# Refining the keys' norms once per head and token, and spreading them to channels by TensorE

## The chip, the cores and the metric

One core of a Trainium2 chip runs the whole program. The metric is device microseconds from start to end of one execution, as the median of several runs; lower is better. TensorE (PE in the rows) multiplies matrices from SBUF into PSUM, VectorE (DVE) and ScalarE (ACT) work on both memories, GpSimd (POOL) on SBUF, and SyncE (SP) issues most of the transfers.

## What is computed

The kernel runs two layers of a backbone over 1024 latent and 256 context tokens. The part that matters here is in the second layer, ahead of a recurrence (RWKV-7): each head's keys, 64 channels wide, are scaled by `k_k` and divided by their norm over those 64 channels.

```python
k = token_shift_mix(k, mu[1])
kk = heads(k * k_k).astype(jnp.float32)
kk = kk / jnp.maximum(jnp.sqrt(jnp.sum(kk * kk, axis=-1, keepdims=True)), 1e-12)
...
    s_fin, o = wkv_scan(r_h, heads(decay), k_d, v_h, -kk, kk * a_h, init, reverse=(d == 1))
```

There are 8 heads, so one norm per head and token: 8 x 1280 numbers.

## The kernel before, in words

Channels lie on partitions and tokens along the row, so a tile of 128 partitions holds a pair of heads (64 channels each) and 1280 columns: 1024 latent tokens, then 256 of the context. The stage `odd_in` goes over four such pairs, j = 0 to 3. For each pair, `dense` projects keys, values and receptances (i = 0, 1, 2). A dense block is 24 matmuls, eight triples of a split-precision product (`hi`/`lo` weights and inputs, one `wl` and two `wh` rows in the trace); blocks are 512, 512 and, for keys and values, 256 columns wide. After the four pairs come four more projections of 1024 columns (`ex` in the rows), each ended by `gates`: load a gate from memory, multiply (L1037), store (`ZCD`).

For each projected tile `shift` mixes neighbouring tokens: GpSimd adds the two neighbours into a buffer `both` (L1061), VectorE scales and adds (L1063, L1066). Then `keys(j)` makes the normalised keys `kkm`, and `prep(j, u)` prepares five chunks of 256 tokens, u = 4, 0, 1, 2, 3, in that order: low-rank products on TensorE (L1149, L1160), a tanh on ScalarE (L1153), cumulative sums on VectorE (L1171 to L1173), products with `kkm` (L1194, L1223, L1224), transposes of the results on TensorE (L1299) with a copy of half of them by VectorE (L1309), and for u < 4 the bonus: VectorE's product L1236, a sum over channels on TensorE (L1241), VectorE's product L1243.

In `keys` ScalarE squares the scaled keys into `sq`. TensorE multiplies by `oblk`, a matrix with two blocks of 64x64 ones: the sums of squares come out 64 times over, once on each channel's partition (L1106). VectorE clips them into `ss` (L1098). ScalarE takes an approximate reciprocal root of all 128x1280 (L1113), and one step of refinement follows, two ScalarE passes (L1115, L1119) and three VectorE passes (L1117, L1121, L1124), each over 128x1280. Last, VectorE multiplies by the key and `k_k` (L1128).

The order of the instructions on each engine isn't the order of the source. A planner (`Lists`) runs the generators against its own clock when the program is built: each `yield "D", 1400` names an engine (P, A, D, G, S) and a cost in ns, `"R"` takes a buffer from a pool and `free` gives it back, `"E"` and `"J"` wait for an event or a job. Jobs of a lower priority number go first; `dense` has 100, so dense products fill what the others leave of TensorE. Each engine then runs its list strictly in order. The recurrence after this stage, `scan`, is planned by a planner of its own, with its own clock. `shift` and `keys` share one buffer `ss`: for i = 0 `shift` doesn't give it back, and `keys` does, after L1121. `pw` is a pool of two PSUM banks that sums and low-rank products share.

## Time and profile before

| | |
|---|---|
| median of three runs | 1558.96 us (1555.4 to 1561.5) |
| the profiled execution | 1569.38 us, span 1567.6 us |
| mean granted TensorE clock | 0.938 of 2.4 GHz |
| busy: TensorE, VectorE, ScalarE, GpSimd | 89%, 64%, 40%, 42% of the span |
| the stage `odd_in`, from its first low-rank products to its last gating product | about 583 to 936 us |

Busy shares are means over the whole span, and the profiled execution is one execution among others; it took 10.4 us more than the median. Matmuls overlap, so the durations of two that follow each other add up to more than the time from start to start.

### The profile page before, as it was taken

To read this page: it belongs to the slowest core of one execution; us is meant where nothing else is said; L and a number is where in the kernel's file an instruction comes from. 1 tells how busy PE (TensorE), PEld (TensorE's weight loads), DVE (VectorE), ACT (ScalarE), POOL (GpSimd) and SP (SyncE) were. 2 spreads that over 40 slices of the span, in tenths; PEclk is the share of its full clock that TensorE was granted. 3 is DMA by queue.
4 is the path that set the end of the run, shared out by engine and by line. 5 is a ranking of instruction groups with operands and counts; after the bars stand their busy time and mean duration, and the time that the engine had idled before them with its cause. 6 is when DMAs were issued, how large, how long until landed. Compare 5 with 4: busy or idle time off the path is not lost. (4 is left out here: it accounts for less than half of the span.)

```text
span 1567.6 us, 32131 instructions
## 1 busy us (share of the span) xinstructions
PE 1393.9 (89%) x12820; PEld 1092.7 (70%) x12820; DVE 1006.2 (64%) x1681; ACT 621.7 (40%) x1242; POOL 662.7 (42%) x925
## 2 busy tenths in 40 slices
PE   6899999999999998987988878898997988886996
PEld 1488888888888786865766656676775766674775
DVE  3746544347513732499999974878497677688567
ACT  2541111111423533445655521343454543557534
POOL 1352424252644532355565522755566246406004
PEclk9999999999999999999999989899998987878999
DMA  7413223222333112244544666655555566674233
GB/s 264 148 65 126 95 89 121 94 81 95 97 132 128 55 44 76 69 139 148 188 135 144 210 215 160 147 164 139 155 142 138 161 158 166 200 236 125 76 94 108
DMA packets 167894, 208.72 MB, mean 133 GB/s; under 512 B 38112, under 2 KB 129632, under 8 KB 167616
## 3 DMA queue, kind: packets, MB, share of 16 engines
q1 hardware_dynamic: 166448, 205.09, 43.4%
q8 instruction: 101, 1.65, 0.5%
q10 hardware_dynamic: 1296, 1.57, 0.3%
q14 instruction: 49, 0.40, 0.1%
HBM read 149.20 MB, written 55.44 MB: 131 GB/s over the span
## 5 line engine op out<-in xcount | busy, mean ns | idle before, releaser
L302 PE MATMUL d<-sx,wh 128*128 128x512 f32 x1152 | 361.6, 395 | 2.5 <-DVE sx L527 1.4
L302 PEld LDWEIGHTS d<-sx,wh 128*128 128x128 f32 x1152 | 217.2, 189 | 53.2 <-POOL sx L397 1.8
L302 PE MATMUL d<-sx,wl 128*128 128x512 f32 x576 | 229.8, 399 | 4.5 <-DVE u L822 2.7
L1396 POOL TENSOR_TENSOR tmp<-X,Bc 128x120 f32<-128x120 f32 (+2 forms) x300 | 122.1, 407 | 204.1 <-DMA Bc<-ED 181.9
L268 POOL TENSOR_TENSOR wl<-wr,wh 128x1024 fp32r<-128x1024 f32 x37 | 95.5, 2582 | 185.7 <-ACT wh L267 176.2
L992 PE MATMUL d<-sx,wh 128*128 128x512 f32 x512 | 167.5, 409 | 0.0
L1936 PE MATMUL d<-sx,wh 128*128 128x512 f32 x384 | 142.5, 439 | 0.0
L1397 POOL TENSOR_TENSOR X<-X,tmp 128x120 f32<-128x120 f32 (+2 forms) x300 | 120.1, 400 | 23.5
L302 PEld LDWEIGHTS d<-sx,wl 128*128 128x128 f32 x576 | 108.9, 189 | 29.7 <-issue 3.3
L628 DVE SCALAR_TENSOR_TENSOR junk<-wra,cb 128x1024 bf16<-128x1024 f32 x56 | 91.5, 1635 | 52.1 <-DMA wra<-in_ada_o 30.5
L992 PEld LDWEIGHTS d<-sx,wh 128*128 128x128 f32 x512 | 102.3, 200 | 23.9 <-issue 2.9
L992 PE MATMUL d<-sx,wl 128*128 128x512 f32 x256 | 116.2, 454 | 0.0
L302 PE MATMUL d<-sc,wh 128*128 128x256 f32 x576 | 104.1, 281 | 0.0
L1936 PE MATMUL d<-sx,wl 128*128 128x512 f32 x192 | 84.1, 438 | 7.4 <-DVE wl L1910 7.4
L1957 DVE SCALAR_TENSOR_TENSOR acc<-hc,vec,acc 128x960 f32<-128x960 f32 (+14 forms) x120 | 89.3, 769 | 1.1
L302 PEld LDWEIGHTS d<-sc,wh 128*128 128x128 f32 x576 | 88.8, 190 | 1.4
L1936 PEld LDWEIGHTS d<-sx,wh 128*128 128x128 f32 x384 | 75.6, 203 | 16.9 <-issue 0.2
L267 ACT CAST wh<-wr 128x1024 fp32r<-128x1024 f32 x37 | 38.7, 1045 | 117.3 <-PE d L302 86.8
L302 PE MATMUL d<-sc,wl 128*128 128x256 f32 x288 | 81.0, 281 | 0.0
L1498 PE MATMUL sc<-w,bk 64*128 64x128 f32 (+1 forms) x640 | 55.9, 313 | 21.7 <-DMA bk<-BKD 14.1
L1498 PEld LDWEIGHTS sc<-w,bk 64*128 64x128 f32 x640 | 47.0, 212 | 30.2 <-issue 24.9
L1512 DVE TENSOR_TENSOR w<-sc,cstb 64x256 f32<-64x256 f32 x80 | 33.8, 422 | 43.1 <-PE sc L1498 26.4
(380 smaller groups left out, 2909.8 us busy)
## 6 DMA issues: line engine op xcount, KB each, us to landing
wr<-in_in_o SPq DMA_DIRECT2D x32, 512.0 KB
wr<-in_in_e SPq DMA_DIRECT2D x24, 512.0 KB
wra<-in_ada_o SPq DMA_DIRECT2D x24, 512.0 KB
BKD<-bk SPq DMA_DIRECT2D x40, 256.0 KB
BTD<-X SPq DMA_DIRECT2D x20, 512.0 KB
bk<-BKD SPq DMA_DIRECT2D x40, 256.0 KB
Bc<-ED SPq DMA_DIRECT2D x20, 512.0 KB
bkt<-BTD SPq DMA_DIRECT2D x40, 256.0 KB
```

Of the source, the lines that this page charges most:

```text
L267: self.nc.scalar.copy(hi, raw)
L268: self.nc.gpsimd.tensor_tensor(out=lo, in0=raw, in1=hi.bitcast(F32), op=ALU.subtract)
L302: self.nc.tensor.matmul(ps[:, :n], lhsT=w[a][:, k, :], rhs=rhs(src, k, b, c0, n), start=(i == 0), stop=(i == len(seq) - 1))
L628: nc.vector.scalar_tensor_tensor(out=junk, in0=w, scalar=1.0, in1=cb[:, s, :], op0=ALU.mult, op1=ALU.mult, accum_out=dst[:, s:s + 1])
L992: nc.tensor.matmul(ps, lhsT=w[a][:, k, :], rhs=rhs(s, k, b, c0, m), start=(q == 0), stop=(q == len(seq) - 1))
L1396: g.tensor_tensor(out=t, in0=X[:, :, j:j + 1].to_broadcast([128, 8, m]), in1=B[:, j, :, j + 1:16] if j < 8 else B2[:, j - 8, :, j - 7:8], ...
L1397: g.tensor_tensor(out=X[:, :, j + 1:16], in0=X[:, :, j + 1:16], in1=t, op=ALU.add)
L1498: nc.tensor.matmul(ps[h][:, d, i, h:h + 1] if ctx else ps[h][:, d, i], lhsT=bk[R[h], c, d, i], rhs=w[R[h], c, d, sl, i, :], start=True, st ...
L1512: nc.vector.tensor_tensor(out=w[o, c, :, 2 * h], in0=ps[h][o, :, :, h], in1=ma[o].unsqueeze(2).to_broadcast([64, 2, 2, 64]), op=ALU.mult)
L1936: nc.tensor.matmul(ps, lhsT=wt(a, k), rhs=rhs("x", k, b, c0, 512), start=(i == 0), stop=(i == len(seq) - 1))
L1957: nc.vector.scalar_tensor_tensor(out=acc[:, o], in0=hc[:, q], scalar=w, in1=acc[:, o], op0=ALU.mult, op1=ALU.add)
```

## The change

The sums of squares are written once per 16 partitions instead of once per channel. `oblk[:, 48:80]` has 16 columns of ones for the first head and 16 for the second. The 1280 tokens are cut in four quarters of 320, and quarter q goes to partitions 32q to 32q+31 of one PSUM tile of 128x320, in four products. Clip, reciprocal root and refinement then run over 128x320. A new constant `rowsel` (128x128, loaded once) spreads each quarter back to the channels by a product of 32 rows, and the key's scaling reads the result from PSUM, in five pieces, since the fourth quarter crosses the border between latent and context tokens. The shared buffer `ss` is given back by each `shift`. The planner's costs are those of the new pieces.

```diff
+ROWSEL = np.zeros((128, 128), np.float32)
+ROWSEL[0::32, :64] = 1.0
+ROWSEL[16::32, 64:] = 1.0
...
+        rows = cp.tile([128, 128], F32, name="rowsel")
+        nc.sync.dma_start(out=rows, in_=A["rowsel"])
+        NQ = TT // 4
...
-            if i:
-                free("ss")
+            free("ss")
...
-            ss = sp.tile([128, TT], F32, tag="ss", name="ss")
-
-            def clip(o, m, ps):
-                yield "D", 1.04 * m + 65
-                nc.vector.tensor_scalar(out=ss[:, o:o + m], in0=ps, scalar1=1e-24, scalar2=None, op0=ALU.max)
+            yield "R", "pw"
+            ps = psb.tile([128, 512], F32, tag="w", name="ks", bufs=2)[:, :NQ]
+            yield "P", 1500
+            for q in range(4):
+                nc.tensor.matmul(ps[32 * q:32 * q + 32], lhsT=self.cst("oblk")[:, 48:80], rhs=sq[:, NQ * q:NQ * q + NQ], start=True, stop=True)
+            x, y, tmp = [sp.tile([128, NQ], F32, tag=f"kn{i}", name=f"kn{i}") for i in range(3)]
+            yield "D", 400
+            nc.vector.tensor_scalar(out=x, in0=ps, scalar1=1e-24, scalar2=None, op0=ALU.max)
+            free("pw")
+            free("sq")
+            yield "A", 1650
+            nc.scalar.activation(out=y, in_=x, func=AF.Abs_reciprocal_sqrt)
+            yield "A", 340
+            nc.scalar.activation(out=tmp, in_=y, func=AF.Square)
+            yield "D", 400
+            nc.vector.tensor_tensor(out=x, in0=x, in1=tmp, op=ALU.mult)
+            yield "A", 340
+            nc.scalar.activation(out=tmp, in_=x, func=AF.Identity, scale=0.375, bias=self.cst("eps")[:, 3:4])
+            yield "D", 400
+            nc.vector.tensor_tensor(out=tmp, in0=tmp, in1=x, op=ALU.mult)
+            yield "D", 400
+            nc.vector.scalar_tensor_tensor(out=y, in0=tmp, scalar=1.875, in1=y, op0=ALU.add, op1=ALU.mult)
+            yield "R", "kkm"
+            KK[j] = kn = mp.tile([128, TT], F32, tag="kkm", name="kkm", bufs=2)
+
+            def scaled(q, ps):
+                for a, b in ((NQ * q, min(NQ * q + NQ, T)), (max(NQ * q, T), NQ * q + NQ)):
+                    if a < b:
+                        p = 1 + a + (a >= T)
+                        yield "D", 1.04 * (b - a) + 70
+                        nc.vector.scalar_tensor_tensor(out=kn[:, a:b], in0=z[:, p:p + b - a], scalar=ka[:, 8 + j:9 + j], in1=ps[:, a - NQ * q:b - NQ * q],
+                                                       op0=ALU.mult, op1=ALU.mult)
                 free("pw")
             js = []
-            for src, c0, m in BLK:
-                o = c0 + (0 if src == "x" else T)
+            for q in range(4):
                 yield "R", "pw"
-                ps = psb.tile([128, 512], F32, tag="w", name="ks", bufs=2)[:, :m]
-                yield "P", m / 1.2
-                nc.tensor.matmul(ps, lhsT=self.cst("oblk"), rhs=sq[:, o:o + m], start=True, stop=True)
-                js.append(spawn(clip(o, m, ps), 4))
...
+                ps = psb.tile([128, 512], F32, tag="w", name="kr", bufs=2)[:, :NQ]
+                yield "P", 600
+                nc.tensor.matmul(ps, lhsT=rows[32 * q:32 * q + 32], rhs=y[32 * q:32 * q + 32], start=True, stop=True)
+                js.append(spawn(scaled(q, ps), 4))
...
-            nc.scalar.activation(out=kn, in_=ss, func=AF.Abs_reciprocal_sqrt)
...
-            for p, o, m in SEG[0]:
-                yield "D", 1.04 * m + 130
-                nc.vector.scalar_tensor_tensor(out=kn[:, o:o + m], in0=z[:, p:p + m], scalar=ka[:, 8 + j:9 + j], in1=kn[:, o:o + m],
-                                               op0=ALU.mult, op1=ALU.mult)
```

The planner makes a new order for the whole stage; the order of `scan` is as before. In the changed program lines of this stage have other numbers: L1106 is the clip, L1114, L1118 and L1120 the refinement, L1129 the scaling, L1103 the sums and L1137 the spreading.

The first place is VectorE's list where the keys of pair 1 get ready, before. The last refinement (L1124) and the scaling (L1128) are followed by a shift (L1063, L1066) and then by the first cumulative sum of pair 1 (L1171).

```order
L1121 TENSOR_TENSOR sq<-sq,ss 128x1280
L1236 SCALAR_TENSOR_TENSOR kb<-kb,vec,Z_4364 128x256
L1309 COPY X<-t_5281 128x8x64
L1124 SCALAR_TENSOR_TENSOR kkm<-sq,kkm 128x1280
L1243 TENSOR_TENSOR kb<-m,Z_4363 128x256
L1128 SCALAR_TENSOR_TENSOR kkm<-Z_4365,ka,kkm 128x1024
L1128 SCALAR_TENSOR_TENSOR kkm<-Z_4365,ka,kkm 128x256
L1063 TENSOR_SCALAR Z_4366<-Z_4366,omu 128x1283
L1066 SCALAR_TENSOR_TENSOR Z_4366<-both,hmu,Z_4366 128x1024
L1066 SCALAR_TENSOR_TENSOR Z_4366<-both,hmu,Z_4366 128x256
L1171 TENSOR_SCALAR thw<-thw 128x2x4x64
```

The same place on VectorE after the change. L1320 is the copy of the transposes, L1069 and L1072 the shift, L1247 and L1254 the bonus, L1182 the first preparation step of pair 1.

```order
L1320 COPY X<-t_5255 128x8x64
L1069 TENSOR_SCALAR Z_4368<-Z_4368,omu 128x1283
L1129 SCALAR_TENSOR_TENSOR kkm<-Z_4367,ka,kr 128x320
L1072 SCALAR_TENSOR_TENSOR Z_4368<-both,hmu,Z_4368 128x1024
L1129 SCALAR_TENSOR_TENSOR kkm<-Z_4367,ka,kr 128x320
L1072 SCALAR_TENSOR_TENSOR Z_4368<-both,hmu,Z_4368 128x256
L1129 SCALAR_TENSOR_TENSOR kkm<-Z_4367,ka,kr 128x320
L1247 SCALAR_TENSOR_TENSOR kb<-kb,vec,Z_4366 128x256
L1129 SCALAR_TENSOR_TENSOR kkm<-Z_4367,ka,kr 128x64
L1129 SCALAR_TENSOR_TENSOR kkm<-Z_4367,ka,kr 128x256
L1254 TENSOR_TENSOR kb<-m,Z_4365 128x256
L1182 TENSOR_SCALAR thw<-thw 128x2x4x64
```

The shift now stands between the pieces of the scaling, ahead of its last three, and the bonus's product (L1254) stands directly before the preparation. The place looks the same for pairs 2 and 3.

On TensorE the last of pair 3's four spreading products (L1137) is followed by one dense triple, the bonus's sum of the pair before (L1252), another triple and the first low-rank products of the new pair (L1160). There is one dense triple between every two spreading products as well. Where pairs 1 to 3 begin, the list holds, between the bonus's sum of chunk 2 and the transposes of chunk 3 of the pair before, 7 triples of 256 columns and 4 of 512.

```order
L1137 MATMUL kr<-kn_6389,rowsel 128x320
L998 MATMUL d<-sx_102,wl 128x512
L998 MATMUL d<-sx_103,wh 128x512
L998 MATMUL d<-sx_102,wh 128x512
L1252 MATMUL m<-kb,cstt 128x256
L998 MATMUL d<-sx_104,wl 128x512
L998 MATMUL d<-sx_105,wh 128x512
L998 MATMUL d<-sx_104,wh 128x512
L1160 MATMUL w<-HS_4357,WS 128x256
L1160 MATMUL w<-HS_4358,WS 128x256
```

Before, no spreading stood here: the low-rank products came directly after the bonus's sum for pairs 1 and 3, and seven triples behind it for pair 2.

The end of the stage on TensorE before: the last bonus's sum (L1241), three dense triples, and the first product of `scan` (L1936).

```order
L1241 MATMUL m<-kb,cstt 128x256
L992 MATMUL d<-sx_112,wl 128x512
L992 MATMUL d<-sx_113,wh 128x512
L992 MATMUL d<-sx_112,wh 128x512
...
L992 MATMUL d<-sx_116,wl 128x512
L992 MATMUL d<-sx_117,wh 128x512
L992 MATMUL d<-sx_116,wh 128x512
L1936 MATMUL d<-sx_102,wl 128x512
```

And after the change: the last bonus's sum is L1252, and the first product of `scan` L1947. Only the first and the last of the dense triples between them are shown.

```order
L1252 MATMUL m<-kb,cstt 128x256
L998 MATMUL d<-sx_106,wl 128x512
L998 MATMUL d<-sx_107,wh 128x512
L998 MATMUL d<-sx_106,wh 128x512
...
L998 MATMUL d<-sx_116,wl 128x512
L998 MATMUL d<-sx_117,wh 128x512
L998 MATMUL d<-sx_116,wh 128x512
L1947 MATMUL d<-sx_102,wl 128x512
```

There are 14 dense triples (42 matmuls) between the last bonus's sum and `scan` now, where there were three. On VectorE, two of the gating half-steps (L1027 of before) and one gating product (L1037 of before) have moved from ahead of the last bonus product to behind it.

## Rows read from the trace of the kernel before

**Rows 1.** The first lines of the profile's page: the span, and VectorE's line of the engine table (busy us, share of the span, instructions).
```profile
span 1567.6 us, 32131 instructions
...
PE 1393.9 (89%) x12820; PEld 1092.7 (70%) x12820; DVE 1006.2 (64%) x1681; ACT 621.7 (40%) x1242; POOL 662.7 (42%) x925
```

**Rows 2.** Busy time of each engine in four stretches of the preparation of the recurrence (us from the span's start), with the number of instructions that start in it, then TensorE's granted clock as a share of 2.4 GHz, the DMA engines' share and GB/s.
```profile
660.00:680.00 20.00, 15.36 (x66) 12.24 (x65) 19.69 (x21) 8.18 (x16) 12.57 (x7) 0.91 0.19 59
720.00:740.00 20.00, 12.35 (x63) 9.72 (x62) 19.39 (x20) 9.16 (x15) 11.64 (x7) 0.83 0.45 150
860.00:880.00 20.00, 16.07 (x79) 12.89 (x78) 18.82 (x27) 8.62 (x18) 9.16 (x8) 0.83 0.47 131
920.00:940.00 20.00, 12.34 (x61) 9.50 (x60) 11.49 (x18) 3.54 (x6) 3.25 (x5) 0.85 0.57 189
```

**Rows 3.** The chain of work that ended last, where it leaves the preparation: start us, us, what.
```profile
925.86 0.35 DVE ar L1224
...
930.59 4.34 DMA ex<-GD
935.02 1.24 DVE ex L1037
936.28 0.32 SPq L1039
...
948.15 0.66 PE sc L1498 x8
```

**Rows 4.** VectorE's instructions on the tiles `ss` and `kkm` and on two lines that read PSUM: line, operation, times it ran; shortest, median and longest duration in ns; first and last start; forms.
```profile
L1098 DVE TENSOR_SCALAR ss<-ks x12: 406/676/693, 648.6 to 833.1; 128x512 f32<-128x512 f32 x8, 128x256 f32<-128x256 f32 x4
...
L1117 DVE TENSOR_TENSOR ss<-ss,sq x4: 1479/1756/3654, 655.4 to 843.0; 128x1280 f32<-128x1280 f32 x4
...
L1128 DVE SCALAR_TENSOR_TENSOR kkm<-Z,ka,kkm x8: 474/1296/2802, 662.1 to 860.5; 128x1024 f32<-128x1024 f32 x4, 128x256 f32<-128x256 f32 x4
...
L1243 DVE TENSOR_TENSOR kb<-m,Z x16: 409/418/425, 700.7 to 928.6; 128x256 f32<-128x256 f32 x16
...
L1027 DVE SCALAR_TENSOR_TENSOR ex<-ex,d x8: 659/678/689, 871.0 to 931.4; 128x512 f32<-128x512 f32 x8
```

**Rows 5.** VectorE's instructions in order of time, and one of ScalarE (start us, us, engine, line, operation, out<-in, form, times; idle time before and what ended it).
```profile
658.33 2.18 DVE L1121 TENSOR_TENSOR sq<-sq,ss 128x1280 f32<-128x1280 f32 x1 [1.44 <-ACT sq L1119]
...
662.07 3.56 DVE L1128 SCALAR_TENSOR_TENSOR kkm<-Z,ka,kkm 128x1024 f32<-128x1024 f32 x2
...
664.65 0.84 ACT L1153 ACTIVATE thw<-w,hw 128x256 f32<-128x256 f32 x2 [3.12 <-PE w L1149]
...
666.46 1.68 DVE L1066 SCALAR_TENSOR_TENSOR Z<-both,hmu,Z 128x1024 f32<-128x1024 f32 x2
...
668.05 0.42 DVE L1171 TENSOR_SCALAR thw<-thw 128x512 f32<-128x512 f32 x1
...
716.40 0.47 DVE L1236 SCALAR_TENSOR_TENSOR kb<-kb,vec,Z 128x256 f32<-128x256 f32 x1
...
726.32 0.68 DVE L1309 COPY X<-t 128x512 f32<-128x512 f32 x1
...
858.57 1.30 DVE L1128 SCALAR_TENSOR_TENSOR kkm<-Z,ka,kkm 128x1024 f32<-128x1024 f32 x1
```

**Rows 6.** VectorE's costliest groups between 610 and 935 us, the lines that the change removes (busy us, mean ns of one | idle time before).
```profile
L1128 DVE SCALAR_TENSOR_TENSOR kkm<-Z,ka,kkm 128x1024 f32<-128x1024 f32 (+1 forms) x8 | 11.0, 1407 | 0.1
...
L1124 DVE SCALAR_TENSOR_TENSOR kkm<-sq,kkm 128x1280 f32<-128x1280 f32 x4 | 9.5, 2379 | 0.0
...
L1117 DVE TENSOR_TENSOR ss<-ss,sq 128x1280 f32<-128x1280 f32 x4 | 8.6, 2161 | 4.2 <-ACT sq L1115 4.2
...
L1098 DVE TENSOR_SCALAR ss<-ks 128x512 f32<-128x512 f32 (+1 forms) x12 | 6.9, 592 | 4.7 <-PE ks L1106 4.7
...
L1121 DVE TENSOR_TENSOR sq<-sq,ss 128x1280 f32<-128x1280 f32 x4 | 6.6, 1654 | 1.9 <-ACT sq L1119 1.9
```

**Rows 7.** TensorE's matmuls in order of time (columns as in rows 5; an fp32 product of the program is two instructions, L992's dense triple is one of `wl` and two of `wh`).
```profile
647.57 1.02 PE L1106 MATMUL ks<-sq,cstt 128*128 128x512 f32 x2
...
648.66 0.63 PE L992 MATMUL d<-sx,wh 128*128 128x512 f32 x2
...
649.13 1.02 PE L1106 MATMUL ks<-sq,cstt 128*128 128x512 f32 x2
...
854.88 0.79 PE L1241 MATMUL m<-kb,cstt 128*128 128x256 f32 x2 [4.11 <-DVE kb L1236]
...
855.89 1.06 PE L992 MATMUL d<-sx,wh 128*128 128x512 f32 x2
...
857.17 1.06 PE L992 MATMUL d<-sx,wh 128*128 128x512 f32 x2
...
915.50 0.71 PE L1299 MATMUL t<-cstt,bk 64*128 64x64 f32 x16
...
916.14 0.50 PE L992 MATMUL d<-sx,wl 128*128 128x512 f32 x1
...
926.85 0.63 PE L992 MATMUL d<-sx,wh 128*128 128x512 f32 x2
...
927.55 0.62 PE L992 MATMUL d<-sx,wh 128*128 128x512 f32 x2
...
928.01 0.59 PE L1241 MATMUL m<-kb,cstt 128*128 128x256 f32 x2
```

16 lines of the change are left out of this document (1 added, 15 removed).

## The prediction

> **What bounds the kernel now.** The profile's first lines give the span, 1567.6 us, and an engine table in which no engine stands out for this change: VectorE is busy 64% of the span [rows 1]. That share is a mean over stages, so the next view is the table of windows over the stage that the change touches, the preparation of the recurrence (some 608 to 936 us). There VectorE is busy 19.69, 19.39 and 18.82 us of 20 in three windows, TensorE only 12 to 16 [rows 2]: here VectorE is the limit, and TensorE, whose instructions run in a fixed order, stands and waits for it. In the last window both fall off; that is the hand-over to the scan. Then the chain that ended last: it leaves the stage through VectorE (925.86), a load of a gate (930.59), the last gating product (935.02 to 936.26), its store on SP (936.28) and the scan's first product (948.15) [rows 3]. Everything after 936.26 is in an order that the change leaves alone, so a last gating product that comes earlier by x should bring the end earlier by x.
>
> **What is removed and added on VectorE.** For each of four head pairs the eight instructions are, undisturbed: three clips (0.69 twice, 0.41), three of 128x1280 at 1.48 (I take L1117's shortest for all three), and the scaling of the keys, 1.30 and 0.47 [rows 4, 5]. Together 8.0 us. The new nine aren't in this trace. Products with one input in PSUM took 0.41 for 256 elements and 0.68 for 512 [rows 4], so I estimate 0.48 for 320 and 0.21 for 64. One clip, three refinements and three scalings of 320, and the pieces of 64 and 256: 7 x 0.48 + 0.21 + 0.41 = 4.0 us. So **4.0 us per pair** is saved.
>
> The old ones in fact took 6.9 + 8.6 + 6.6 + 9.5 + 11.0 = 42.6 us [rows 6], not 4 x 8.0 = 32: 10.6 us were stretch, 2.5 of it in the first pair (2.18 for a product of 1.48, 3.56 for the scaling's 1.77) [rows 5] and 8.1 in the later three. Whether it goes with the instructions or falls on their neighbours is unknown: 0 to 2.7 us per later pair. L1128, with both tensors in SBUF, reached 2802 ns, while L1243 and L1027, with one in PSUM, never left 409 to 425 and 659 to 689 [rows 4]. The new scalings are of the second kind, the refinements of the first, so I take half, **1.35 us per later pair**. The Trainium skill (SBUF — State Buffer, "Who interferes with whom") says that VectorE and GpSimd take a shared port pair as an exclusive lock, and that a VectorE instruction with at most one SBUF input doesn't contend; the trace agrees in kind. By that rule GpSimd's holds stay and the stretch would move on, and the sum would be 3 x 1.35 = 4 us smaller; by the rows, had they all gone with the instructions, 4 us larger.
>
> **The start.** The first pair is a latency, since nothing else is ready. Now the first step of the preparation on VectorE (L1171) starts at 668.05, after the tanh at 664.65 and the values' shift at 666.46 [rows 5]. In the new order TensorE does, from 647.57: four sums, two triples of dense products, eight of the context's half-width triples, two more, four spreading products with three triples between, three more, then the low-rank product ahead of the tanh. An fp32 product of 512 columns with three dense ones takes 1.56 us (647.57 to 649.13) and three dense ones alone 0.70 (926.85 to 927.55) [rows 7], so 0.86 for 512 columns and 0.54 for 320. That is 2.15 + 1.4 + 2.8 + 1.4 + 4.25 + 2.1 = 14.1, so 661.7, then some 0.45 to the tanh and 0.95 to VectorE: 663.1. The refinement itself (one table load and seven short steps) ends near 654, before TensorE gets to the spreading, and the shift is done by about 659.5, because it no longer waits for the squares' buffer. **Gain 4.9 us**; bounds 2 (the shift is late as now) and 6.
>
> **The later pairs.** Here the order costs something. Before, two shifts' products stand between the finished keys and the next preparation; in the new order they stand ahead of the last scalings, and after the bonus product (L1243 of before) nothing is left to do. From the end of the product ahead of it: the bonus's sum 0.43 (256 fp32 columns, half of 0.86), a triple 0.70, the low-rank product 0.24 (a third of a triple), the tanh's 0.84 [rows 5] and hand-overs of 0.45 (my estimate) make 2.65 us, of which VectorE has work for 1.0. Idle: 1.65. Two smaller ones: VectorE's copy of the transposes waits for TensorE, which has 7 half-width and 4 full triples (5.3 us), the bonus 0.43 and the transposes 0.64 [rows 7] to do after the same product, 6.9 with hand-overs, while VectorE's own way there, 716.40 to 726.32 now [rows 5], shrinks by some 3 us to 6.6 from that product's end: 0.3 idle, and 0.3 more at the fourth spreading. So **2.2 us idle per later pair**; bounds 0.5 (as now) and 5. Net per pair 4.0 + 1.35 - 2.2 = 3.15, three times: **9.5**.
>
> TensorE's own bill is the four spreading products, 4 x 0.54 = 2.15 us per pair (the sums cost what they did: 1280 columns). It has room: 4 to 8 us idle in 20 [rows 2]. If the cover were gone it would cost 8.6. Switching between products of 32, 64 and 128 rows: 64-row transposes among dense products start and end within about 0.1 us of them (915.50 to 916.14, 16 of them) [rows 7], so ten switches per pair are 1 us at most, hidden the same way. The Trainium skill (TensorEngine Tiling (Array Packing), "Key Properties") warns that a change of tiling mode drains TensorE; the row prices such a drain at 0.1, which leaves the sum as it is. ScalarE saves some 3 x 0.9 us per pair and isn't the limit. The extra 64 KB load runs at the stage's start, where VectorE is idle.
>
> **The tail.** In the new order 42 dense products (14 triples) stand behind the last bonus on TensorE, not 9. From the bonus at 928.01 [rows 7] to the last gating product's end there were 8.25 us now (3 of them for the gate's load); then 0.43 + 14 x 0.70 + about 0.9 for ScalarE and hand-overs + 0.68 + 1.24 = 13.0. Against that, two gating steps of 0.68 and one of 1.24 move from ahead of the bonus to behind it: 2.6. **Loss 2.2 us**; bounds 0 and 12 (all 14 triples at the lower clock, 1.28 each).
>
> **Sum.** 4.9 + 9.5 - 2.2 = 12.2 us. The profiled execution took 1569.38 us (span 1567.6), so 1557; it lay 10.4 above the median of the runs, 1558.96, from which the same gain gives 1547.
>
> **Rivals.**
> *All the stretch goes, the idle is hidden.* 3 x (4.0 + 2.7 - 0.5) + 5.5 - 1 = 23: 1536. For it: the old steps were among the most stretched [rows 6]. Against it: GpSimd has as much to do as before.
> *TensorE's fixed order gives it back.* If the idle at each pair's end is 5 us instead of 2.2 and the start brings 2, the sum is 3 x 0.35 + 2 - 2.2 = 1: 1558. For it: the new order has no filler there. Against it: idle on VectorE lets GpSimd through unhindered, which lowers stretch later.
> *Slower: the pair's end at half clock.* After a wait of 4.11 us TensorE's triples took 1.28 us, not 0.70 (855.89 to 857.17) [rows 7], 1.2 and not 2.4 GHz. If each bonus comes after such a wait, the eleven triples behind it take 10.6 us, not 5.3, and the spreading doubles its 4.25: idle of 2.2 + 5.3 + 2 = 9.5 per pair, and 3 x (5.35 - 9.5) + 4.9 - 2.2 = -10: 1569. It decides from 6.3 us idle per pair, where the gain is nothing; from 8.9 the loss can be measured. Against it: the granted clock was 0.83 to 0.91 over the windows that waited [rows 2], so the lower level held for 4 to 7 us of 20 there.
> *It changes nothing,* because the scan's start hangs on something else: the chain goes through the last gating product without a gap [rows 3], so I give this little, inside the second rival.
>
> **How the numbers follow.** A measurement of this kernel tells about 0.5% (7.8 us) from no change. Chances: forecast (8 to 18 us) 0.50, all of the gain 0.14, given back 0.27, slower 0.09. So faster 0.64, same 0.27, slower 0.09. The time is the forecast's, 1547. The range runs from just under the first rival's time, 1535, to the second's, 1558; outside it stay the slower case and a little of each other.
>
> **What would show it.** In the new profile: nine short instructions per pair at 0.2 to 0.5 us with hardly any stretch on those that read PSUM; L1171's successor first at about 663; one idle of 1 to 2 us on VectorE before each pair's first preparation, put down to ScalarE's tanh; the last gating product 12 us earlier, preceded by TensorE's dense run. The prediction is wrong if VectorE waits 5 us or more at the copy of the transposes or ahead of the preparation, or if the low clock falls on the 14 triples.

## The result: 1.4% slower, and where the profile shows it

The changed kernel takes 1581.6 us (median of 4 runs, 1577.4 to 1585.1) against 1559.3 before: a ratio of 1.0138, 95% interval 1.0113 to 1.0162. Run again later, beside other runs of before, it was 1.0119 (1.0088 to 1.0149). The prediction said 1547, with a range of 1535 to 1558; both are missed. The first lines of its profile, as in [rows 1]: VectorE did lose 14.2 us of work, TensorE is busy 21 us longer.

```profile
span 1581.3 us, 32207 instructions
...
PE 1414.8 (89%) x12860; PEld 1095.3 (69%) x12860; DVE 992.0 (63%) x1685; ACT 612.5 (39%) x1242; POOL 650.4 (41%) x925
```

The windows of [rows 2], now. In the second and the third VectorE is busy 11 us of 20, where it had been 19, and TensorE is busy 18 at a granted clock of 0.66. The places have changed: VectorE waits for a TensorE that runs slowly.

```profile
660.00:680.00 20.00, 18.93 (x104) 15.10 (x103) 15.38 (x20) 12.36 (x25) 8.18 (x6) 1.00 0.36 109
720.00:740.00 20.00, 17.88 (x48) 10.76 (x49) 10.96 (x19) 5.04 (x9) 1.62 (x3) 0.66 0.31 95
860.00:880.00 20.00, 17.85 (x58) 10.18 (x57) 11.63 (x15) 4.51 (x8) 5.19 (x4) 0.66 0.38 112
920.00:940.00 20.00, 17.21 (x101) 13.40 (x100) 15.01 (x22) 5.40 (x11) 8.16 (x7) 1.00 0.80 229
```

TensorE's matmuls at the border between the first pair and the second, in order of time (columns as in [rows 7]; L1137 is the spreading, L998 the dense triples, L1252 the bonus, L1160 the low-rank product of the next preparation).

```profile
718.01 0.63 PE L998 MATMUL d<-sx,wh 128*128 128x512 f32 x2
722.12 1.43 PE L1137 MATMUL kr<-kn,rowsel 32*128 32x320 f32 x2 [3.49 <-DVE kn L1120]
723.48 0.80 PE L998 MATMUL d<-sx,wl 128*128 128x512 f32 x1
...
725.06 1.43 PE L1137 MATMUL kr<-kn,rowsel 32*128 32x320 f32 x2
...
728.00 1.43 PE L1137 MATMUL kr<-kn,rowsel 32*128 32x320 f32 x2
...
733.75 1.05 PE L1252 MATMUL m<-kb,cstt 128*128 128x256 f32 x2
...
735.72 0.40 PE L1160 MATMUL w<-HS,WS 96*128 96x256 f32 x2
```

TensorE stands still for 3.49 us until the refinement's last step is done. Then a spreading product with its triple takes 2.94 us (722.12 to 725.06), and the low-rank product that the next pair begins with comes 13.60 us after the first of them. I had reckoned 1.24 for product and triple. About the same stretch at the three borders in the view by windows (columns as in [rows 2]), and the 9.28 us behind the first of them: over the borders TensorE is never idle and the granted clock is 0.51, the lower of its two levels, and behind the low-rank product it is back at 1.00.

```profile
722.12:735.72 13.60, 13.60 (x25) 7.20 (x26) 6.07 (x11) 1.87 (x2) 0.00 (x0) 0.51 0.38 116
794.00:807.50 13.50, 13.50 (x26) 7.11 (x27) 5.97 (x11) 1.87 (x2) 0.00 (x0) 0.51 0.39 117
866.00:879.20 13.20, 13.20 (x26) 6.82 (x26) 5.66 (x11) 1.87 (x2) 0.00 (x0) 0.51 0.39 119
...
735.72:745.00 9.28, 9.28 (x48) 7.51 (x46) 7.71 (x11) 7.15 (x15) 4.84 (x5) 1.00 0.21 60
```

VectorE at the second border: between its short instructions it waits each time for a product, and at last for the tanh behind the low-rank product, 8.7 us in all with the 1.20 ahead of these rows.

```profile
801.25 0.55 DVE L1129 SCALAR_TENSOR_TENSOR kkm<-Z,ka,kr 128x320 f32<-128x320 f32 x1 [2.00 <-PE kr L1137]
...
804.19 0.67 DVE L1129 SCALAR_TENSOR_TENSOR kkm<-Z,ka,kr 128x64 f32<-128x64 f32 x2 [2.00 <-PE kr L1137]
806.62 0.42 DVE L1254 TENSOR_TENSOR kb<-m,Z 128x256 f32<-128x256 f32 x1 [1.76 <-PE m L1252]
808.76 0.43 DVE L1182 TENSOR_SCALAR thw<-thw 128x512 f32<-128x512 f32 x1 [1.72 <-ACT thw L1164]
```

Taken from the start of each pair's first step of preparation (L1171 before, L1182 after, and its counterpart in the other kernels), the stage divides like this, in us. "Start" runs from the first sum of squares, the tail to the end of the last gating product.

| profile | start | pair 1 to 2 | 2 to 3 | 3 to 4 | tail |
|---|---|---|---|---|---|
| before | 20.5 | 67.9 | 66.1 | 66.5 | 67.7 |
| before, a second time | 20.5 | 69.2 | 66.8 | 66.1 | 63.1 |
| changed | 17.3 | 72.9 | 71.7 | 71.7 | 68.6 |
| changed, a second time | 17.3 | 73.2 | 72.3 | 71.4 | 70.7 |

From means of the two profiles each: 3.2 gained at the start, 5.1 lost at each of three borders, 4.2 lost in the tail, 16.4 us lost in all.

The second profile of before is there because the medians differ by 22 us and the first two profiles by 13.7 only.

> The kernel before, unchanged, for a second profile. In the two profiles the changed kernel's stage of preparation ended 12.8 us later, while the medians differ by 22. If the first profile of before had a slow scan, this one shows its stage ending at 936 again, its scan's part 10 us shorter than the 620 us there, and a time near 1559. If not, the changed kernel's scan is itself slower than that of before.

It took 1555.7 us, with a stage that ends at 933.9 instead of 936.3, and 608.5 us from the scan's first product to the end, where the first had 620.1; the changed kernel's two have 621.3 and 612.7. So the scan varies by up to some 12 us between executions of one program, and the stage holds what can be pinned down: 16.4 of the 22 us by which the medians differ.

> The changed kernel, unchanged, for a second profile and a ratio from the same chip as the others. Expected: a ratio of 1.014, the half clock at each of the three borders again, the stage's end 12 to 14 us behind that of before. If the half clock at the borders were chance, it would be missing here at one of them or more, and that pair would be some 5 us shorter.

All three borders were slow again, the granted clock 0.50, 0.53 and 0.53. At the second and the third TensorE came out of the standstill at full clock and fell to half within the first turn, which took 2.30 and 2.18 us; all turns behind it took 2.94.

### The profile page after: what moved, and what is told of

It is laid out like the page before. It is cut to its first block, busy times and chain, and to the rows that moved or that the text cites. A ratio compares the mean times of both kernels' runs of the same rounds, so it can differ in the third digit from the quotient of the medians.

```text
span 1581.3 us, 32207 instructions
## 1 busy us (share of the span) xinstructions
PE 1414.8 (89%) x12860; PEld 1095.3 (69%) x12860; DVE 992.0 (63%) x1685; ACT 612.5 (39%) x1242; POOL 650.4 (41%) x925
## 3 DMA queue, kind: packets, MB, share of 16 engines
q10 hardware_dynamic: 1296, 1.57, 0.3%
## 5 line engine op out<-in xcount | busy, mean ns | idle before, releaser
L998 PE MATMUL d<-sx,wh 128*128 128x512 f32 x512 | 167.5, 409 | 0.0
L1947 PE MATMUL d<-sx,wh 128*128 128x512 f32 x384 | 140.7, 434 | 1.6 <-issue 1.6
L998 PE MATMUL d<-sx,wl 128*128 128x512 f32 x256 | 117.3, 458 | 0.0
L998 PEld LDWEIGHTS d<-sx,wh 128*128 128x128 f32 x512 | 102.0, 199 | 21.5 <-issue 2.2
L1947 PE MATMUL d<-sx,wl 128*128 128x512 f32 x192 | 84.3, 439 | 4.4 <-DVE wl L1921 4.4
L1947 PEld LDWEIGHTS d<-sx,wh 128*128 128x128 f32 x384 | 75.0, 202 | 18.6 <-issue 2.2
L1202 POOL TENSOR_TENSOR kd<-kd,Z 128x512 f32<-128x512 f32 x20 | 28.5, 1426 | 128.5 <-DVE kd L1198 128.5
L1509 PE MATMUL sc<-w,bk 64*128 64x128 f32 (+1 forms) x640 | 56.8, 317 | 22.1 <-DMA bk<-BKD 17.6
```

Source lines behind the costliest of these rows:

```text
L998: nc.tensor.matmul(ps, lhsT=w[a][:, k, :], rhs=rhs(s, k, b, c0, m), start=(q == 0), stop=(q == len(seq) - 1))
L1202: nc.gpsimd.tensor_tensor(out=kd, in0=kd, in1=bc2(kT[:, z]), op=ALU.mult)
L1509: nc.tensor.matmul(ps[h][:, d, i, h:h + 1] if ctx else ps[h][:, d, i], lhsT=bk[R[h], c, d, i], rhs=w[R[h], c, d, sl, i, :], start=True, st ...
L1947: nc.tensor.matmul(ps, lhsT=wt(a, k), rhs=rhs("x", k, b, c0, 512), start=(i == 0), stop=(i == len(seq) - 1))
```

## Experiments on the half clock

Ratios are to the kernel before on the same chip, with a 95% interval. Line numbers of these kernels differ from the changed kernel's by a few lines, up or down.

**Keep TensorE busy.**

```diff
-                ps = psb.tile([128, 512], F32, tag="w", name="kr", bufs=2)[:, :NQ]
+                pw_ = psb.tile([128, 512], F32, tag="w", name="kr", bufs=2)
+                ps = pw_[:, :NQ]
                 yield "P", 600
+                if j and q == 0:
+                    for r in range(15):
+                        nc.tensor.matmul(pw_, lhsT=WS[:, r % 4, 0:128], rhs=HS[r % 4][:, 0:512], start=True, stop=True)
                 nc.tensor.matmul(ps, lhsT=rows[32 * q:32 * q + 32], rhs=y[32 * q:32 * q + 32], start=True, stop=True)
```

> The changed kernel with 15 discarded products of 512 columns put on TensorE ahead of the first spreading product of each later pair, where it now stands still for 3.5 us. Nothing else moves. Theory A, the clock: the four spreading products and the single triples between them are slow because they come after that standstill and run at 1.2 GHz (1.36 and 1.58 us); kept busy, they run at 2.4 GHz (0.73 and 0.70), the way from the first spreading product to the next pair's first low-rank product falls from 13.6 us to about 7.2, VectorE's idle time there from 8.7 us to about 2.3, and the time by some 3 x 6.3 = 19 us, to 1563. Theory B, the order: what costs is that spreading product and scaling take turns behind one another with nothing else left to do; the clock is only a sign of it, and the time stays within 5 us of 1582. If the discarded products themselves hold the spreading up, it is above 1582.

Measured: 1564.1 us, 1.0009 (0.9982 to 1.0035), as theory A said. TensorE at the first border, in order of time:

```profile
719.05 3.60 PE L1140 MATMUL kr<-HS,WS 96*128 96x512 f32 x15
722.58 0.80 PE L1141 MATMUL kr<-kn,rowsel 32*128 32x320 f32 x2
...
724.20 0.80 PE L1141 MATMUL kr<-kn,rowsel 32*128 32x320 f32 x2
```
And the window from the first spreading product to the low-rank product:
```profile
722.58:730.12 7.54, 7.54 (x27) 4.24 (x26) 4.82 (x10) 1.87 (x2) 0.00 (x0) 1.00 0.68 209
```

3.6 us of work whose results are thrown away make the kernel some 18 us faster: 1.62 us per turn, not 2.94, and 7.54 us for the way, not 13.60. The order of the instructions is otherwise the same, so the clock is the cause of the loss against before.

**Spread over 128 rows, then 64.** The selector gets 512 columns (256), a block per quarter that is zero outside the quarter's rows, and the product reads all of `y` (half of it).

```diff
-                nc.tensor.matmul(ps, lhsT=rows[32 * q:32 * q + 32], rhs=y[32 * q:32 * q + 32], start=True, stop=True)
+                nc.tensor.matmul(ps, lhsT=rows[:, 128 * q:128 * q + 128], rhs=y, start=True, stop=True)
```

> The changed kernel with each spreading product over all 128 rows of the norms, with a selector that is zero in 96 of them, instead of over its 32 rows. Same order, same columns, same result. Theory A1, few rows: the half clock at each pair's end comes from products that use 32 of the 128 rows; with 128 rows the granted clock is back at 2.4 GHz within the spreading, and the time falls towards 1563. Theory A2, the standstill ahead: the half clock comes from the wait of 3.5 us before the first of them, the products stay at 1.36 us each, and the time stays within 5 us of 1582.

Measured: 1563.1 us, 1.0001 (0.9971 to 1.0031). The standstill is still there, and the clock comes back within the border. The second border:

```profile
782.88 1.43 PE L1138 MATMUL kr<-kn,rowsel 128*128 128x320 f32 x2 [2.22 <-DVE kn L1121]
...
785.38 1.07 PE L1138 MATMUL kr<-kn,rowsel 128*128 128x320 f32 x2
...
786.98 0.70 PE L1138 MATMUL kr<-kn,rowsel 128*128 128x320 f32 x2
...
788.21 0.70 PE L1138 MATMUL kr<-kn,rowsel 128*128 128x320 f32 x2
```

2.50 us for the first turn, 1.23 for the third, which is the prediction's 0.54 + 0.70. So the standstill alone doesn't keep the half clock for a whole border: theory A2 is out, and A1 looked right.

> The changed kernel with each spreading product over 64 rows (a selector that is zero in 32 of them), between the changed kernel's 32 (1582) and the version with 128 (1563). The order is the same, and like the changed kernel it goes between products of fewer rows and dense ones of 128 rows four times a border. Theory A1, few rows hold the clock down: with twice the rows the granted clock comes back earlier within the border, and the time lies between, below 1573. Theory A3, it is the going between tile sizes: it is still there, the half clock lasts as long as with 32 rows, and the time stays at 1577 to 1585.

Measured: 1577.6 us, 1.0096 (1.0059 to 1.0133), no better than 32 rows. At the first border TensorE came out of the standstill at full clock and lost it on the way, as the changed kernel did at two borders of its second profile:

```profile
721.91 0.80 PE L1139 MATMUL kr<-kn,rowsel 64*128 64x320 f32 x2 [2.13 <-DVE kn L1121]
...
723.54 0.80 PE L1139 MATMUL kr<-kn,rowsel 64*128 64x320 f32 x2
...
725.71 1.43 PE L1139 MATMUL kr<-kn,rowsel 64*128 64x320 f32 x2
...
728.65 1.43 PE L1139 MATMUL kr<-kn,rowsel 64*128 64x320 f32 x2
```

At full clock a turn takes 1.63 us with 64 rows as with 32, at half clock 2.94 with both. What the two have in common, and 128 rows have not, is the going between tile sizes.

**Go between sizes for nothing.** The version with 128 rows, and behind each product a discarded one of 32 rows and 16 columns.

```diff
...
                 nc.tensor.matmul(ps, lhsT=rows[:, 128 * q:128 * q + 128], rhs=y, start=True, stop=True)
+                nc.tensor.matmul(pw_[:, NQ:NQ + 16], lhsT=rows[32 * q:32 * q + 32, 128 * q:128 * q + 128], rhs=y[32 * q:32 * q + 32, :16], start=True, stop=True)
```

> The version with spreading products over all 128 rows, and behind each of them one discarded product over 32 rows and 16 columns, so that TensorE goes to the small tile and back four times a border as in the changed kernel, while the spreading itself stays on 128 rows. Theory A1, few rows: 16 columns on 32 rows are next to nothing, the clock comes back as with 128 rows alone, and the time is that version's 1563 plus at most 4 us for the products themselves. Theory A3, the going between tile sizes: the half clock stays for the whole border as with 32 and with 64 rows, and the time is 1577 or more.

Measured: 1578.4 us, 1.0111 (1.0072 to 1.0151): theory A3 by the time, and A1 falls. At the first border, in order of time, and then the window from the first spreading product to the low-rank one:

```profile
721.54 1.43 PE L1139 MATMUL kr<-kn,rowsel 128*128 128x320 f32 x2 [3.46 <-DVE kn L1121]
722.91 0.60 PE L1140 MATMUL kr<-kn,rowsel 32*128 32x16 f32 x2
...
724.89 1.27 PE L1139 MATMUL kr<-kn,rowsel 128*128 128x320 f32 x2
```
```profile
721.54:733.79 12.25, 12.25 (x33) 7.99 (x34) 6.07 (x11) 1.87 (x2) 0.00 (x0) 0.63 0.41 128
```

Four products of 16 columns lengthen the way from the 7.79 us that it took with 128 rows alone (716.92 to 724.71) to 12.25, with the clock at 0.63; at the other two borders it is 0.70 and 0.64. Not all of that is the clock: in the first pair, at full clock, the same way takes 8.42 us with them and 6.33 without, so 2.1 us per border, 6 in all, are their own, where the expectation allowed 4. Of the 15 us by which this version is slower than the one with 128 rows alone, 9 are left for A3. The changed kernel needs both conditions: the discarded work kept the going between sizes and had no standstill, 128 rows kept the standstill and didn't go between sizes, and each has the time of before. What is not separated is the change of size from one more short product per turn: a discarded one of 16 columns over all 128 rows wasn't run. That 64 rows are as slow as 32, with as many products as with 128, speaks for the size.

**All four at once.** The four products are issued in a row, into two of the small PSUM banks and two dense ones.

```diff
...
+            for q in range(4):
+                yield "R", ("pw", "psd")[q // 2]
...
+            yield "P", 2400
+            for q in range(4):
+                nc.tensor.matmul(kps[q], lhsT=rows[32 * q:32 * q + 32], rhs=y[32 * q:32 * q + 32], start=True, stop=True)
```

> The changed kernel with the four spreading products issued one behind another, into two of the small PSUM banks and two of the dense ones, instead of each with one dense triple behind it into two small banks in turn. Theory A, the clock: they still come after the wait, at 1.2 GHz, 4 x 1.36 = 5.4 us, and four triples of 1.28 stand ahead of the low-rank product: 10.6 us and not 13.6, so 3 us less per pair, 9 in all: 1573. Theory B, the order: the turns are gone, VectorE's idle time of 8.7 us per pair falls to about 2, and the time to 1562.

Measured: 1557.5 us, 0.9973 (0.9951 to 0.9995), 24 us under the changed kernel, more than either theory gave. Its first two borders:

```profile
722.00 1.45 PE L1139 MATMUL kr<-kn,rowsel 32*128 32x320 f32 x8 [3.49 <-DVE kn L1120]
723.38 0.80 PE L998 MATMUL d<-sx,wl 128*128 128x512 f32 x1
...
790.53 0.82 PE L1139 MATMUL kr<-kn,rowsel 32*128 32x320 f32 x8 [0.90 <-DVE kn L1120]
791.28 0.50 PE L998 MATMUL d<-sx,wl 128*128 128x512 f32 x1
```

Four products over different rows take about as long as one in a turn: 1.38 us at half clock, 0.75 at full. There is one change of tile size and back; at the first border the half clock lasts some 5 us, at the second, behind a standstill of 0.90 us, it doesn't come, and at the third it is there again, with a granted clock of 0.71 over the 5.58 us to the low-rank product.

**Earlier keys.** `keys` and the shift that it waits for at rank 5.5, not 7.

> The changed kernel with one number of the planner changed: the keys of a later pair and the shift that they wait for get rank 5.5 and not 7, so that the norms and the spreading stand among the preparations of the pair before, not behind the last of them. Theory C, too late: what costs is that nothing is left to do beside the spreading; with work on both sides the idle 8.7 us per pair go, whatever the clock: 1582 - 26 = 1556 or less, and VectorE is over 95% busy across the pairs' borders. Theory A, the clock: the spreading still follows waits on VectorE and halves the clock; VectorE then waits for TensorE elsewhere, and the time stays over 1570.

Measured: 1571.8 us, 1.0055 (1.0022 to 1.0089). That is over theory A's 1570, but so little that the interval reaches to both sides of it, and the profile shows some of each theory. The order is another at each border; the windows over the spreading at the second and the third:

```profile
778.65:785.00 6.35, 6.22 (x35) 3.35 (x34) 6.29 (x9) 1.94 (x3) 6.12 (x6) 1.00 0.00 0
849.58:861.90 12.32, 12.32 (x23) 6.18 (x24) 5.51 (x10) 1.86 (x2) 2.77 (x2) 0.51 0.41 130
```

The pair around the first of them takes 63.1 us, the one around the second 73.1: one program, the same instructions, both clocks. No standstill stands ahead of the first, one of 1.57 us ahead of the second. At the first border the turns were slow too (2.94 us each behind the first): a standstill of 3.51 us ended 1.35 us ahead of them, at the bonus's sum. But preparations of the old pair stood beside them, and the pair took 65.5.

## Experiments on the other half

With the clock restored the time is that of before, not 12 us less. VectorE's idle time by cause over the three later pairs (658.87 to 858.76 in the version with 128 rows, 668.7 to 870.8 in the second profile of before): line, tiles, times | busy, mean | idle before.

```profile
L1183 DVE TENSOR_SCALAR thw<-thw 128x512 f32<-128x512 f32 x16 | 12.6, 790 | 7.3 <-ACT thw L1165 7.3
L1130 DVE SCALAR_TENSOR_TENSOR kkm<-Z,ka,kr 128x320 f32<-128x320 f32 (+2 forms) x15 | 6.9, 479 | 4.8 <-PE kr L1138 4.6
L1255 DVE TENSOR_TENSOR kb<-m,Z 128x256 f32<-128x256 f32 x12 | 5.1, 423 | 5.6 <-PE m L1253 5.6
L1115 DVE TENSOR_TENSOR kn<-kn,kn 128x320 f32<-128x320 f32 x3 | 3.5, 1171 | 2.8 <-ACT kn L1113 2.8
```
```profile
L1309 DVE COPY X<-t 128x512 f32<-128x512 f32 x15 | 10.1, 672 | 2.9 <-PE t L1299 2.9
L1187 DVE TENSOR_SCALAR kd<-ta,ka 128x512 f32<-128x512 f32 x15 | 8.0, 535 | 1.1 <-ACT ta L1166 1.1
L1243 DVE TENSOR_TENSOR kb<-m,Z 128x256 f32<-128x256 f32 x11 | 4.6, 417 | 1.0 <-PE m L1241 0.8
```

By subtraction of busy time from these pairs' length, VectorE idles 2.9 us a pair before, 6.6 with 128 rows, 11.9 in the changed kernel. Of the changed kernel's, 5.3 go with the clock; 3.6 more than before are left without it, and I put them down to the order. The version with discarded work, at full clock over the whole border, agrees: 6.8 us a pair.

**Is VectorE the limit at all?** Before, with the three refining instructions of 128x1280 left out on VectorE.

> The kernel before, in its order, with the three refining instructions of 128x1280 per pair left out on VectorE (the keys' norms are then the first estimate only); ScalarE's part of the refinement stays. In three later pairs they took 7.2 + 4.4 + 8.0 = 19.6 us of VectorE, in the first pair 5.2. Theory F, VectorE is the limit of this stage: nearly all of it comes off, 1562 - 20 = 1542. Theory G, it is not, and whatever is taken from VectorE turns into idle time there: 1555 or more. In between, the share that arrives tells how much the prediction's 4.0 us per pair could have brought.

Measured: 1547.0 us, 0.9903 (0.9869 to 0.9937): 15 of the 24.8 us that the three took on VectorE arrive, with the interval 10 to 20. VectorE is the limit here for some 60% of what is taken from it, if the order holds still. The prediction counted 100%.

**One part alone.** Every shift frees the buffer of sums; the keys' sums get their own. Nothing else.

> The kernel before with one part of the change alone: every shift frees its buffer of sums at once, and the keys' sums of squares have a buffer of their own. Norms, refinement and scaling are on 128x1280 as before. By the prediction the values' shift of the first pair no longer waits for the keys there, worth up to 2 us at the start, and the later pairs don't change: a time 0 to 3 us under the kernel before. If this part, and not the norms, disturbs the later pairs, it is slower than before by 5 us or more.

Measured: 1558.6 us, 0.9975 (0.9954 to 0.9996). It isn't this part that costs.

**Take the new waits out.** `four_k5` below is the version with four in a row and `keys` at rank 5.5; `late` and `late4` move one wait, in the changed kernel and in the version with four in a row:

```diff
-            yield "E", ("kk", j)
             yield "E", "stack"
...
             note(("EF", j, u))
             yield "J", jr
+            yield "E", ("kk", j)
...
```

> The version with four spreading products in a row, and with the keys of later pairs at rank 5.5 instead of 7 (their shift stays at 7), so that the refinement's short steps stand ahead of the last preparations' steps on VectorE. What is open: at full clock (the version with discarded products) the pairs still take as long as before the change, 66.9 us, although VectorE is busy 4 us less in each; its idle time grew from 2.9 to about 6.5 us a pair. Theory D, the refinement is late: TensorE waits 3.49 us for its last step (in the first border), and all that follows is late by that; with the refinement ahead that wait is under 1 us, the clock does not fall, VectorE's idle time is back at 3 us a pair, and the time falls from 1557.5 to about 1548. Theory E, the order ends each pair without filler whatever the refinement does: idle time stays at 5 to 6 us a pair, and the time within 4 us of 1557.5.

Measured: 1558.6 us, 0.9976 (0.9953 to 0.9999). Theory E: the idle time is there as before, only elsewhere.

> The changed kernel with one wait moved: a preparation waits for the finished keys only where it first uses them, behind its exponentials, so that its low-rank products, its tanh and its sums can stand in a border beside the spreading, which still goes in turns with single dense triples. Theory E, the order without filler: of VectorE's idle time in three pairs the 7.6 us ahead of the sums go, 1582 - 8 = 1574, and the half clock stays. Theory A, standstill and turns: if six triples ahead of the first spreading product instead of one cover its wait, the clock holds too, and the time falls to 1555 or less.

Measured: 1577.3 us, 1.0109 (1.0062 to 1.0156). The wait ahead of the sums falls (from 9.4 to 3.1 us over the stage), and the waits for the spreading grow (from 18.5 to 22.1). The half clock stays at two borders, where TensorE stood still for 2.85 and 2.22 us right or almost right ahead of the turns. At the third 6 us of other products stand between a standstill of 2.58 us and the turns, and they run at full clock throughout (875.85 to 885.40, granted 1.00, 1.63 us a turn): the second condition again, within one program.

> The same wait moved in the version with the four spreading products in a row. The 7.3 us that VectorE waited ahead of the sums in three pairs should go from that version's 1557.5: 1550. Against it stands a longer tail: 20 dense triples behind the last bonus product instead of 10, some 4 us by the prediction's rule for the tail if VectorE is ready before them: then 1554. Theory E would be wrong if the time does not fall below 1556 although the idle time ahead of the sums is gone.

Measured: 1560.0 us, 0.9978 (0.9956 to 0.9999). The idle time ahead of the sums is gone, and the time didn't fall: VectorE waits instead, from 664 us to the stage's end, for the refinement's steps on ScalarE (11.0 us) and for GpSimd (6.8).

**The refinement on one engine.** Five short VectorE instructions, no ScalarE between them.

```diff
-            nc.scalar.activation(out=tmp, in_=y, func=AF.Square)
...
+            nc.vector.tensor_tensor(out=tmp, in0=x, in1=y, op=ALU.mult)
+            nc.vector.tensor_tensor(out=x, in0=tmp, in1=y, op=ALU.mult)
+            nc.vector.tensor_scalar(out=tmp, in0=x, scalar1=0.375, scalar2=-1.25, op0=ALU.mult, op1=ALU.add)
```

> The version with four spreading products in a row, and with the refinement's two ScalarE steps done by three short VectorE instructions instead, so that from the first estimate on the refinement stays on one engine. It adds some 0.8 us of VectorE per pair and takes away two hand-overs each way. If the refinement's hand-overs hold the border up (VectorE's waits for ScalarE there, 2.4 us in three pairs, and TensorE's standstill behind them, 3.49 in the first border), the time falls from 1557.5 to about 1551; a tail of 20 dense triples and not 10 may cost up to 4 of it. If the order gives it back elsewhere, it stays at 1555 to 1560.

Measured: 1559.6 us, 0.9990 (0.9968 to 1.0011). By itself it brings nothing either.

**All of them.**

> All four edits: four spreading products in a row, the keys at rank 5.5, the refinement on VectorE alone, and the wait for the finished keys only where they are first used. By theory F each of the waits so removed comes off: ahead of the sums 2.5 us, in the refinement 1 to 3 us a pair; with the 4 us a pair saved on VectorE the stage ends some 15 us earlier than before the change, and the time is 1547. If VectorE's idle time is as large as with each edit alone, 6 us a pair, the time is 1556 to 1561 like theirs.

Measured: 1549.4 us, 0.9934 (0.9897 to 0.9971), and once more:

> The version with four edits once more, for a closer interval: 0.993 of the kernel before expected, 0.990 to 0.997.

1553.0 us, 0.9922 (0.9894 to 0.9951). This version beats both kernels. Its pairs, taken here from second chunk to second chunk since the first one now begins early, take 64.8, 63.4 and 62.2 us, against 65.7, 66.1 and 67.9 before; the whole stage takes 272.3 against 288.7 and 285.7. Each of the other three edits, added by itself to the four products in a row, had moved the wait to another place; together they leave, over its three pairs, one large wait, for GpSimd:

```profile
L1246 DVE SCALAR_TENSOR_TENSOR kb<-kb,vec,Z 128x256 f32<-128x256 f32 x12 | 10.6, 884 | 9.1 <-POOL kb L1242 9.1
```

Whether the changed norms have a share in that:

> The kernel before with one edit: a preparation waits for the finished keys only where it first uses them. Its norms are as before, on 128x1280. If the gain of the version with four edits (13 us under the kernel before) comes from this wait, it is here as well: 1549 or less. If it comes from the 4 us a pair that the changed norms save, with the waits only standing in its way, this one stays within 5 us of the kernel before, since there VectorE hardly waits at a border (1.0 to 2.9 us in three pairs in any one place).

Measured: 1562.6 us, 1.0009 (0.9984 to 1.0035). The later wait does nothing in the kernel before, so it alone isn't the gain. That it is the shorter work on VectorE that pays, once the waits are out of its way, fits but isn't shown: the other edits, the keys' rank above all, were not tried in the kernel before. Over the stage VectorE is busy 237 us in the version with four edits, 246 in the changed kernel and 260 before, so 9 of its 23 us less came with the later edits and not with the shorter norms. Moving GpSimd's sum ahead to remove the last large wait cost what it should have brought:

> The version with four edits, and GpSimd's sum for the bonus as soon as its inputs are there, not behind the reading vectors' product. VectorE waited 10.5 us for it over the stage. If VectorE limits the stage, up to that comes off: 1540 to 1546; if GpSimd then holds up the reading vectors' product by as much, nothing changes: 1549.

Measured: 1561.5 us, 0.9987 (0.9961 to 1.0012). It was a new order for the whole stage, and I didn't follow up which of its waits is to blame.

## Why the prediction was wrong, step by step

By the sum, in us gained: the start 3.2 for 4.9, the three later pairs -15.3 for 9.5, the tail -4.2 for -2.2. The step that failed is the later pairs' idle time.

**The start: right in kind, 3.2 us and not 4.9.** The sums of squares took 0.7 us, not 2.15, and the eight half-width and the other triples stood behind them as I had it. But from the first spreading product to the low-rank product it took 7.77 us, not 6.35, since a turn took 1.63, and from there to VectorE's first step 2.96, not 1.4: ScalarE loads the table of the tanh behind the low-rank product now. Before, that was over when the product came, at 664.21. The load after, where the product came at 661.22, and before:

```profile
662.01 1.28 ACT L1164 ACT_TABLE_LOAD   x1
```
```profile
660.25 1.28 ACT L1153 ACT_TABLE_LOAD   x1
```

**VectorE's saving: 4 us a pair as predicted, the stretch not.** VectorE's busy time in a later pair fell from 63.9 to 60.2 us, in the second profiles from 64.4 to 60.1. I had added half of the stretch, 1.35. It moved on: the refinement's second product, 0.49 undisturbed, took 2.04 on average (1.22 in the second profile), and of the steps that the change leaves alone some grew and some shrank. Two of VectorE's groups between 640 and 950 us after, and the counterpart of the first of them before:

```profile
L1234 DVE SCALAR_TENSOR_TENSOR ar<-kkm,E 128x256 f32<-128x256 f32 x20 | 28.4, 1420 | 0.0
L1118 DVE TENSOR_TENSOR kn<-kn,kn 128x320 f32<-128x320 f32 x4 | 8.2, 2038 | 0.6 <-ACT kn L1116 0.6
```
```profile
L1223 DVE SCALAR_TENSOR_TENSOR ar<-kkm,E 128x256 f32<-128x256 f32 x20 | 21.3, 1067 | 0.0
```

Here the rule of the Trainium skill that I had weighed (SBUF — State Buffer, "Who interferes with whom") was the better guide than my half: with its sum, 4 us smaller, this term is right. That the stretch is GpSimd's doing no run here shows; none took GpSimd's work away.

**The later pairs' idle: the step that failed.** I set 2.2 us a pair; it became 9.0 more than before (11.9 against 2.9), which turns a net gain of 3.15 a pair into a loss of 5.1. Two things in that step were wrong. First, "ten switches per pair are 1 us at most, hidden the same way" put the going between tile sizes at next to nothing. That priced a change of tile size from a block of 16 transposes, which goes there and back once, at full clock. At full clock a change costs twice that price: 1.63 against 1.23 for a turn is 0.2 per change. The Trainium skill's warning (TensorEngine Tiling (Array Packing), "Key Properties") that a change of mode drains TensorE agrees in kind with these 0.2. What I didn't see, and my row couldn't show, is that four such turns behind a standstill run at 1.2 GHz, 2.94 each; that takes 5.3 of the 9.0. Second, the hand-over: I counted the bonus, a triple, the low-rank product and the tanh, and left out that the refinement's last step is itself late, so that TensorE stands for 2.15 to 3.49 us ahead of the first product, and that product and scaling take turns in the planner's order, with two small banks for four products.

**The rivals.** The slower one was the nearest: half clock at the pair's end behind a standstill, and 9.5 us of idle per pair against the 9.0 measured. But the size is luck. It put 5.3 of its 9.5 on the eleven triples between the bonus's sum of chunk 2 and the transposes; these ran at a granted clock of 1.00, 0.77 and 0.77 at the three borders, and VectorE's waits for the transposes behind them come to 1.2 us over the stage. The half clock lay behind them, on the spreading's turns, which it had priced at 2 and which cost 6.1 (13.60 against 7.54 us), and it didn't have the going between tile sizes that keeps it there. Its sum of 10 us lost falls short of the stage's 16.4 by the stretch (3 x 1.35), the tail and the start; the rest up to the medians' 22 lies outside the stage. I gave it 9%, because the lower level had held only 4 to 7 us in a window before. That was read from a stage without the new products. Behind it the second rival was waiting: with the clock restored the idle time is still 3.6 us a pair above before, where it had put 5, and the gain is given back, at 1563 beside a before of 1562.

**The tail: right in size for its dense run.** The 42 products took 9.81 us at full clock, as 14 x 0.70 said. The chain there:

```profile
936.22 0.43 PE m L1252 x2
936.65 9.81 PE d L998 x42
946.49 0.61 ACT ex L1031
```

From the bonus to the last gating product's end it took 13.0 us, as I had it. Loss 2.2 predicted, 4.2 as a mean of two profiles each, and the two profiles of before differ by more than that (67.7 and 63.1). My upper bound of 12 doesn't follow from its own terms: 14 triples at 1.28 and not 0.70 add 8.1 to the 2.2.

## What to carry to other kernels

Before giving TensorE many small products, look at what stands around them: issue products over different rows in a row, or pad them to full rows, but don't let them take turns with full-size ones behind a wait. Where the engine that limits a stage loses work, the order around it decides how much arrives: here 60% with the order held still, next to nothing with a new one, and a time 10 to 12 us under before when the waits at the border had been taken out all together, part of which may be the order's. A window whose busy engine isn't the one that was busy before, with the granted clock beside it, shows both.

## What the runs showed of the hardware

- Behind a standstill of 2.1 to 3.5 us, four products of 32 rows in turns with dense triples ran at 1.2 GHz nearly throughout, for 13 us and more with TensorE busy: at six borders in two profiles of the changed kernel the granted clock was 0.50 to 0.53, and at two of them it fell only within the first turn. With 64 rows it was 0.61, 0.52 and 0.52. Products of 128 rows at the same place were back at 2.4 GHz after some 4 us at two borders and 6 at the third; with a discarded product of 32 rows and 16 columns behind each of them the granted clock was 0.63, 0.70 and 0.64 over the border. Without a standstill the same turns ran at 2.4 GHz throughout (1.00 over 7.54 us), and so they did where 6 us of other products stood between a standstill and them (1.00 over 9.55 us).
- Going between 32 and 128 rows cost 0.2 us per change at full clock (1.63 against 1.23 for a turn), and as much with 64 rows.
- Four fp32 products over four groups of 32 rows, issued in a row, took 0.75 us at full clock, as long as one alone in turns (0.73). The Trainium skill (TensorE: Matmul & The Clock Gate, "Part 3: Packing small matmuls") gives 3.07 times for four such tiles of 512 columns. Here it is 3.9 against four turns' products, each of which pays for two changes of size, and 2.9 against four products of 128 rows at 0.54 (1.24 for a turn less 0.70 for its triple).
- Between executions of one program, the scan took 608.5 and 620.1 us before, 612.7 and 621.3 in the changed kernel, which leaves its order alone. So two single profiles can differ by some 12 us without a change.
